# A hybrid decoder step: a buffer for each raw weight chunk of the first projection group, and the squares of later input tiles split and tied to copies of transposed columns

## The chip, the cores and the metric

The kernel runs on one core of a Trainium2 chip. The metric is the device time of one execution in microseconds (us); smaller is better. Engines are named as in the profile: PE multiplies matrices and transposes through the matrix unit, PEld loads its weights, DVE is the vector engine, ACT the activation engine, POOL the general engine, and SP issues most DMA transfers. An engine works through its own list of instructions in order, and an instruction that waits holds back all that stand behind it on that engine.

## The reference, cut to what matters

One layer of a decoder with two kinds of attention heads. Only its beginning matters here: all rows (16 learned meta tokens, 1024 prompt tokens, 32 sample tokens) are normalized and multiplied by a wide input matrix.

```python
def rms_norm(x, g):
    xf = x.astype(jnp.float32)
    var = jnp.mean(xf * xf, axis=-1, keepdims=True)
    return (xf * lax.rsqrt(var + EPS) * g.astype(jnp.float32)).astype(x.dtype)
...
    h = rms_norm(x, norm_pre_g[l])
    u = h @ w_in          # 2048 x 7184; columns 2048 on are the values "sv"
```

Everything after that (stick-breaking attention over prompt and paged cache, gated linear attention, gates, the output projection) is not touched by the change.

## The kernel before, in words

**The start.** The 1072 rows are nine tiles of up to 128 rows and 2048 columns: x0 to x7, each loaded as two halves of 1024 columns (512 KB a half, L207 and L212), and the small x8 with 112 rows (L209, L210). The halves share 11 buffers (tag "x"), so the twelfth half and later ones wait until a transposition has finished with an older half. Each tile goes through norm_x (L215): ACT squares it into a scrap area with a running sum (L225; halves of 1024 columns for x0 to x4, quarters of 512 for x5 to x7, four pieces of 256 for x8), DVE adds up the partial sums (L227), rstd_ (L156) makes the reciprocal root in a chain of one DVE operation (L162), two ACT operations (L163, L164) and four DVE operations (L165 to L168), and DVE scales both halves in place (L236).

**Three column chunks.** `CHUNKS` cuts the rows into 0 to 383, 384 to 767 and 768 to 1071, three x tiles each. For each chunk c and each of 16 blocks k of 128 columns, PE transposes three 128x128 pieces into one PSUM bank tx (L260; five banks, so the sixth waits until the first is emptied), ACT copies the bank into the high part of hT with the gain gpre (L261), and DVE subtracts to get the low part (L262), which empties the bank. hT holds the whole normalized input, transposed, for the rest of the projections.

**The first weight group.** The product with the first 128 value columns runs along with the transpositions: three matmuls for each c and k (L272 high by high, L273 low by high, L274 high by low). Its weights come as eight chunks of 256x128 (weight_chunk, L177): SP loads the raw chunk into a buffer of tag "wr" (128 KB, L180), ACT rounds it to the high part (L184), DVE subtracts to the low part (L185). Tag "wr" has 3 buffers in the pool wp, which serves the weight chunks of all later groups too, so the fourth raw chunk waits until the first has been subtracted. The next group, wr_k, uses the same tag and the inproj loop (L289 to L291).

**What sets the order.** A scheduler turns the program into one list per engine. Loads and weight chunks are marked urgent. Where the later tiles are normalized is written out by hand: `NORMS` (L238) says after which (c, k) the whole norm_x of a tile is called, for example tile 3 after (0, 1) and tile 8 after (1, 8). Transfers take turns on eight completion semaphores, so a transfer also waits until the one eight places earlier has landed. Small constants are loaded by `constants` (L139): the attention bias, nbal, a gain and the page table; DVE negates nbal once it has landed (L142).

Other names that the prediction uses: gpre (L133) is the gain, loaded through the ACT queue in 2048 elements of 4 bytes; the load of x7 on SP waits for the last transposition of chunk 0; acc_k at L289 is the first matmul after the three chunks.

Of the kernel before, what the change touches and what calls it, by code (L numbers as in the profile page):

```python
# [10 lines left out]
F32 = mybir.dt.float32  # L11
# [4 lines left out]
AF = mybir.ActivationFunctionType  # L16
# [4 lines left out]
P = 128  # L21
D = 2048
NK = D // P
# [15 lines left out]
C_SQ, C_SK, C_SV, C_SG, C_GQ, C_GK, C_GV, C_GG, C_GA = 0, 1024, 2048, 3072, 4096, 4608, 5120, 6144, 7168  # L39
# [8 lines left out]
NOSYNC = mybir.DependencyInfo(mybir.DependencyClass.NoSync, mybir.DependencyReason.DATA)  # L48
# [34 lines left out]
def hybrid_step(ctx: ExitStack, tc: tile.TileContext, x_prompt, x_sample, cache_k, cache_v, state_gla,  # L83
# [5 lines left out]
    vec, act, pool = nc.vector, nc.scalar, nc.gpsimd  # L89
# [12 lines left out]
    wp = wp_cm.__enter__()  # L102
# [29 lines left out]
    gpre = cst.tile([P, NK], F32, name="gpre")  # L132
# [39 lines left out]
    hT = [slots.tile([P, 2176], F32R, tag=f"s{k}", name=f"hT{k}") for k in range(NK)]  # L172
# [1 line left out]
    hl = [t[:, 1088:1088 + T] for t in hT]  # L174


    def weight_chunk(w, kk, c0, nm, dst=None):  # L177
        with urgent():
            raw = wp.tile([P, 2, P], F32, tag="wr", name=f"wr_{nm}")
            nc.sync.dma_start(raw[:], w[kk * 256:(kk + 1) * 256, c0:c0 + P].rearrange("(k p) c -> p k c", p=P))  # L180
            if dst is None:
                dst = [wp.tile([P, 2, P], F32R, tag=t, name=f"{t}_{nm}")[:] for t in ("wh", "wl")]
            wh, wl = dst
            act.copy(wh, raw[:])  # L184
            vec.tensor_tensor(wl, raw[:], wh.bitcast(F32), ALU.subtract)  # L185
        return wh, wl
# [3 lines left out]
    with tc.tile_pool(name="xp", bufs=2) as xp, tc.tile_pool(name="xps", bufs=5, space=PSUM) as xps:  # L190
        wf = xp.tile([P, 14, P], F32R, tag="wf", bufs=1, name="wf")
        wfl = [stg.tile([P, 2, P], F32R, tag="stg", name=f"wfl{kk}")[:] for kk in range(7)]
        first = [accp.tile([P, 512], F32, tag="acc", name=f"acc_v0_{c}") for c in range(3)]
        wchunks = []
        xts = {}

        def load_x(i):

            xt = [xp.tile([P, H], F32, tag="x", bufs=11, name=f"x{i}_{f}") for f in range(2 if i < 8 else 1)]
            if i == 8:  # L200
                pool.memset(xt[0][32:64], 0.0)
            with urgent():
                for f in range(2):
                    fs = slice(f * H, (f + 1) * H)
                    if i == 0:
                        nc.scalar.dma_start(xt[f][:META], meta_tokens[:, fs])
                        nc.sync.dma_start(xt[f][META:], x_prompt[0, 0:P - META, fs])  # L207
                    elif i == 8:
                        nc.scalar.dma_start(xt[0][64 * f:64 * f + 16], x_prompt[0, SEQ - 16:SEQ, fs])  # L209
                        nc.sync.dma_start(xt[0][64 * f + 16:64 * f + 48], x_sample.rearrange("b t d -> (b t) d")[:, fs])  # L210
                    else:
                        nc.sync.dma_start(xt[f][:], x_prompt[0, i * P - META:(i + 1) * P - META, fs])  # L212
            xts[i] = xt

        def norm_x(i):  # L215
            xt = xts[i]
            rows = P if i < 8 else 112
            w = H if i < 5 else 512 if i < 8 else 256
            q = len(xt) * H // w
            ssq = xp.tile([P, 4], F32, tag="ssq", name=f"ssq{i}")  # L220
            for e in range(q):
                j0 = 0 if i < 5 else (448 if i < 8 else 768) + 1088 * (e % 2)
                jk = hT[15][:rows, j0:j0 + w]
                xe = xt[e * w // H][:rows, e * w % H:e * w % H + w]
                act.activation(jk, xe, AF.Square, accum_out=ssq[:rows, e:e + 1])  # L225
            sq = xp.tile([P, 1], F32, tag="sq", name=f"sq{i}")
            vec.tensor_reduce(sq[:rows], ssq[:rows, :q], mybir.AxisListType.X, ALU.add)  # L227
            if i == 8:
                other = xp.tile([P, 1], F32, tag="so", bufs=1, name="so")
                pool.memset(other[:], 0.0)  # L230
                vec.tensor_copy(other[0:48], sq[64:112])
                vec.tensor_copy(other[64:112], sq[0:48])
                vec.tensor_tensor(sq[:rows], sq[:rows], other[:rows], ALU.add)
            r = rstd_(xp, sq[:rows], D, rows, 1, f"x{i}")
            for t in xt:
                vec.tensor_scalar(t[:rows], t[:rows], r, None, ALU.mult)  # L236

        NORMS = {(0, 1): 3, (0, 4): 4, (0, 10): 5, (1, 2): 6, (1, 5): 7, (1, 8): 8}  # L238
        for i in range(5):
            load_x(i)  # L240
            if i == 2:
                constants()
                for kk in range(NK // 2):
                    dst = (wf[:, 2 * kk:2 * kk + 2, :], wfl[kk]) if kk < 7 else None
                    wchunks.append(weight_chunk(w_in[0], kk, C_SV, f"v0_{kk}", dst))
        for i in range(3):
            norm_x(i)
        for c, (lo, hi) in enumerate(CHUNKS):
            n = hi - lo
            for k in range(NK):  # L250
                ps = xps.tile([P, 384], F32, tag="tx", name=f"tx{c}_{k}")
                ks = slice(k % 8 * P, (k % 8 + 1) * P)
                for j in range(3):
                    xt = xts[3 * c + j]
                    if len(xt) == 2:
                        src, ii = xt[k // 8][:, ks], ident[:]
                    else:
                        rs = slice(64 * (k // 8), 64 * (k // 8) + 48)
                        src, ii = xt[0][rs, ks], ident[rs, rs]
                    nc.tensor.transpose(ps[:, j * P:min((j + 1) * P, n)], src, ii)  # L260
                act.activation(hh[k][:, lo:hi], ps[:, :n], AF.Copy, scale=gpre[:, k:k + 1])  # L261
                vec.scalar_tensor_tensor(hl[k][:, lo:hi], ps[:, :n], gpre[:, k:k + 1], hh[k][:, lo:hi].bitcast(F32),  # L262
                                         ALU.mult, ALU.subtract)
                if c == 0 and k == 7:
                    load_x(5)
                if (c, k) in NORMS:
                    norm_x(NORMS[c, k])
            lo, hi = SCHUNKS[c]
            o_ = first[c][:, :hi - lo]
            for k in range(NK):  # L270
                wh, wl = (t[:, k % 2, :] for t in wchunks[k // 2])
                mm(o_, wh, hh[k][:, lo:hi], start=(k == 0), stop=False)  # L272
                mm(o_, wh, hl[k][:, lo:hi], start=False, stop=False)  # L273
                mm(o_, wl, hh[k][:, lo:hi], start=False, stop=(k == NK - 1))  # L274
            if c == 0:
                for i in (6, 7, 8):
                    load_x(i)
# [1263 lines left out]
```

## Time and profile before

| what | value |
|---|---|
| median of 3 runs | 2123.5 us (2121.63 to 2123.98) |
| span of the profiled execution | 2126.0 us, 2.5 us above that median; no other time of this execution is given |
| busy PE, DVE, ACT | 97%, 74%, 47% of the span |
| mean granted PE clock | 0.993 |
| first transposition on PE | 13.30 us |
| first matmul after the three chunks | 73.61 us |

The profile is read in four views. The page gives shares for the whole span. The table of stretches ("windows") gives the busy time of each engine between two times; an engine whose busy time equals the stretch is the bound there. The view of waits says which engine waited for what. The timeline lists instructions in order: start in us, duration in us, engine, line, operation, output and inputs, count when several like ones are merged, and in brackets the idle time before with what ended it. Rows marked SPq or ACTq are DMA issues, not the transfers themselves.

### The profile page before, as it was taken

What the parts mean: (1) busy time and instruction counts of PE and PEld (TensorE: products, weight loads), DVE (VectorE), ACT (ScalarE), POOL (GpSimd) and SP (SyncE); (2) the same over time, 40 slices, a digit from 0 to 9 for tenths busy, and PEclk for the clock granted to TensorE, in tenths of its full rate; (3) what the DMA queues carried; (4) which work ended last, traced back from release to release, by engine and by line L of the source; (5) the groups of instructions that cost most, each with busy time, mean ns of one, the idle gap of its engine ahead of it and who ended that gap; (6) DMA issues with size and microseconds to landing.
All of it is one profiled execution on the core that took longest, in us unless ns stands there. A gap on an engine that the chain in (4) does not pass through costs nothing.

```text
span 2126.0 us, 43346 instructions
## 1 busy us (share of the span) xinstructions
PE 2062.8 (97%) x12546; PEld 1872.1 (88%) x12546; DVE 1573.4 (74%) x6592; ACT 995.7 (47%) x2536; POOL 81.8 (4%) x298
## 2 busy tenths in 40 slices
PE   5999999999999999999999999999999999999997
PEld 5999999999999989999898998998888897777765
DVE  6368888889888889898798898978544446453575
ACT  7345556565555646434435335353444335342332
POOL 0000000100001000100000000000000000000000
PEclk9999999999999999999999999999999999999999
DMA  6234443544444354554343444335777665452484
GB/s 198 72 99 127 129 127 103 142 127 113 136 130 121 109 138 118 158 137 116 113 128 109 132 122 128 96 86 151 239 225 241 223 192 185 136 153 75 129 285 171
DMA packets 380442, 304.02 MB, mean 143 GB/s; under 512 B 50410, under 2 KB 320682, under 8 KB 380202
## 3 DMA queue, kind: packets, MB, share of 16 engines
q1 hardware_dynamic: 378010, 300.97, 49.0%
q8 instruction: 99, 1.62, 0.3%
q14 instruction: 141, 1.16, 0.2%
q10 hardware_dynamic: 2192, 0.27, 0.1%
HBM read 243.39 MB, written 57.72 MB: 142 GB/s over the span
## 4 chain that ended last, share of the span: by engine, by line
PE 82%; DVE 7%; DMA 6%; ACT 2%; issue 2%; SPq 0%; POOL 0%; ACTq 0%; DVEq 0%; POOLq 0%
PE acc_g L289 4%; PE acc_g L291 4%; PE acc_g L290 4%; PE b L1450 4%; PE b L1451 4%; PE b L1452 4%; PE acc_k L289 3%; PE acc_k L290 3%; PE acc_k L291 3%; PE acc_q L289 3%; PE acc_q L290 3%; PE acc_q L291 3%; PE acc_v L289 3%; PE acc_gv L289 3%; PE acc_gv L291 3%; PE acc_gv L290 3%
## 5 line engine op out<-in xcount | busy, mean ns | idle before, releaser
L384 DVE SCALAR_TENSOR_TENSOR jk<-kp,qb 128x128 f32<-128x128 f32 x2048 | 591.0, 289 | 39.7 <-DMA qb<-qsd 2.3
L289 PE MATMUL acc_g<-hT,wh_g 128*128 128x368 f32 (+2 forms) x768 | 251.3, 327 | 1.3 <-ACT gx L438 1.2
L291 PE MATMUL acc_g<-hT,wl_g 128*128 128x368 f32 (+2 forms) x768 | 248.0, 323 | 0.0
L290 PE MATMUL acc_g<-hT,wh_g 128*128 128x368 f32 (+2 forms) x768 | 247.6, 322 | 0.0
L1450 PE MATMUL b<-ring,f 128*128 128x512 f32 x416 | 166.7, 402 | 6.6 <-ACT gx L438 3.7
L1314 DVE TENSOR_TENSOR ring<-wr,ring 128x512 fp32r<-128x512 f32 x104 | 70.7, 690 | 134.8 <-ACT ring L1313 134.3
L384 DVE DVE_READ_ACCUMULATOR jk<-kp,qb 128x1 f32 x2048 | 166.4, 81 | 0.0
L1451 PE MATMUL b<-ring,f 128*128 128x512 f32 x416 | 163.5, 393 | 0.8 <-DVE ring L1314 0.7
L1452 PE MATMUL b<-ring,f 128*128 128x512 f32 x416 | 163.2, 392 | 0.0
L289 PEld LDWEIGHTS acc_g<-hT,wh_g 128*128 128x128 f32 x768 | 144.7, 188 | 13.1 <-issue 7.3
L291 PEld LDWEIGHTS acc_g<-hT,wl_g 128*128 128x128 f32 x768 | 144.6, 188 | 2.0 <-issue 2.0
L290 PEld LDWEIGHTS acc_g<-hT,wh_g 128*128 128x128 f32 x768 | 144.7, 188 | 0.7
L1313 ACT CAST ring<-wr 128x512 fp32r<-128x512 f32 x104 | 64.4, 622 | 163.0 <-DMA wr<-in_w_out_dram 72.9
L289 PE MATMUL acc_gv<-hT,wh_gv 128*128 128x384 f32 (+1 forms) x384 | 129.2, 337 | 0.0
L289 PE MATMUL acc_k<-hT,wh_k 128*128 128x378 f32 (+1 forms) x384 | 127.6, 332 | 0.0
L290 PE MATMUL acc_k<-hT,wh_k 128*128 128x378 f32 (+1 forms) x384 | 125.4, 326 | 0.0
L289 PE MATMUL acc_q<-hT,wh_q 128*128 128x368 f32 (+2 forms) x384 | 125.3, 326 | 0.0
L291 PE MATMUL acc_gv<-hT,wl_gv 128*128 128x384 f32 (+1 forms) x384 | 125.3, 326 | 0.0
L291 PE MATMUL acc_k<-hT,wl_k 128*128 128x378 f32 (+1 forms) x384 | 125.2, 326 | 0.0
L290 PE MATMUL acc_gv<-hT,wh_gv 128*128 128x384 f32 (+1 forms) x384 | 124.7, 325 | 0.0
L290 PE MATMUL acc_q<-hT,wh_q 128*128 128x368 f32 (+2 forms) x384 | 123.6, 322 | 0.0
L291 PE MATMUL acc_q<-hT,wl_q 128*128 128x368 f32 (+2 forms) x384 | 123.5, 322 | 0.0
(427 smaller groups left out, 5403.5 us busy)
## 6 DMA issues: line engine op xcount, KB each, us to landing
kp<-in_cache_k_dram SPq DMA_DIRECT2D x512, 64.0 KB
vr<-in_cache_v_dram SPq DMA_DIRECT2D x64, 512.0 KB
tf<-in_w_out_dram SPq DMA_DIRECT2D x64, 256.0 KB
qb<-qsd SPq DMA_DIRECT2D x64, 256.0 KB
td<-tf SPq DMA_DIRECT2D x64, 256.0 KB
wr_g<-in_w_in_dram SPq DMA_DIRECT2D x128, 128.0 KB
wr<-td SPq DMA_DIRECT2D x64, 256.0 KB
wr<-in_w_out_dram SPq DMA_DIRECT2D x48, 256.0 KB
```

Of the source, the lines that this page charges most:

```text
L289: mm(acc[c][:, :n], wh[:, k2, :], hh[k][:, lo:hi], start=(k == 0), stop=False)
L290: mm(acc[c][:, :n], wh[:, k2, :], hl[k][:, lo:hi], start=False, stop=False)
L291: W.mark = mm(acc[c][:, :n], wl[:, k2, :], hh[k][:, lo:hi], start=False, stop=(k == NK - 1)).ins
L384: ins = vec.scalar_tensor_tensor(jk[:], kp[:], 1.0, qbs[h, b][:, t, :], ALU.mult, ALU.mult, accum_out=zt[:, t, NPG - 1 - i:NPG - i])
L1313: act.copy(wh, r)
L1314: vec.tensor_tensor(wl, r, wh.bitcast(F32), ALU.subtract)
L1450: mm(bk[:], ah, wh, start=first and k == 0, stop=False, skip_group_check=True)
L1451: mm(bk[:], ah, wl, start=False, stop=False, skip_group_check=True)
L1452: mm(bk[:], al, wh, start=False, stop=last and k == 7, skip_group_check=True)
```

## The change

Two edits, both in the first 74 us. First, each raw chunk of the first weight group gets a buffer of its own: a tag "w0" with 8 buffers in the pool of the start phase, 8 KB more of each partition there; the other groups keep the 3 buffers of tag "wr". Second, the squares leave norm_x for a function of their own. Tiles 0 to 2 are squared as before. For tiles 3 to 8 a table `SQUARES` names, for each (c, k), a tile and the parts of it that are squared there, in two steps for tiles 3 to 7; each square is ordered behind the ACT copy of that (c, k), with an ordering that adds no semaphore wait, since both are on ACT. The rest of norm_x follows after the last part. Sizes of squares and their number stay the same.

```diff
-    def weight_chunk(w, kk, c0, nm, dst=None):
+    def weight_chunk(w, kk, c0, nm, dst=None, raw=None):
         with urgent():
-            raw = wp.tile([P, 2, P], F32, tag="wr", name=f"wr_{nm}")
+            if raw is None:
+                raw = wp.tile([P, 2, P], F32, tag="wr", name=f"wr_{nm}")
...
+        sums_x = {}
+
+        def squares(i, parts, behind=None):
+            xt = xts[i]
+            rows = P if i < 8 else 112
+            w = H if i < 5 else 512 if i < 8 else 256
+            if i not in sums_x:
+                sums_x[i] = xp.tile([P, 4], F32, tag="ssq", name=f"ssq{i}")
+            for e in parts:
+                j0 = 0 if i < 5 else (448 if i < 8 else 768) + 1088 * (e % 2)
+                jk = hT[15][:rows, j0:j0 + w]
+                xe = xt[e * w // H][:rows, e * w % H:e * w % H + w]
+                ins = act.activation(jk, xe, AF.Square, accum_out=sums_x[i][:rows, e:e + 1])
+                if behind is not None:
+                    tc.add_manual_dep(ins.ins, behind.ins.name, NOSYNC, reason="behind")
+
         def norm_x(i):
             xt = xts[i]
             rows = P if i < 8 else 112
-            w = H if i < 5 else 512 if i < 8 else 256
-            q = len(xt) * H // w
-            ssq = xp.tile([P, 4], F32, tag="ssq", name=f"ssq{i}")
-            for e in range(q):
-                j0 = 0 if i < 5 else (448 if i < 8 else 768) + 1088 * (e % 2)
-                jk = hT[15][:rows, j0:j0 + w]
-                xe = xt[e * w // H][:rows, e * w % H:e * w % H + w]
-                act.activation(jk, xe, AF.Square, accum_out=ssq[:rows, e:e + 1])
+            q = len(xt) * H // (H if i < 5 else 512 if i < 8 else 256)
+            ssq = sums_x.pop(i)
...
-        NORMS = {(0, 1): 3, (0, 4): 4, (0, 10): 5, (1, 2): 6, (1, 5): 7, (1, 8): 8}
+        SQUARES = {(0, 2): (3, (0,)), (0, 4): (3, (1,)), (0, 6): (4, (0,)), (0, 8): (4, (1,)), (0, 11): (5, (0, 1)), (0, 13): (5, (2, 3)),
+                   (1, 1): (6, (0, 1)), (1, 3): (6, (2, 3)), (1, 4): (7, (0, 1)), (1, 6): (7, (2, 3)), (1, 8): (8, (0, 1, 2, 3))}
         for i in range(5):
             load_x(i)
             if i == 2:
                 constants()
                 for kk in range(NK // 2):
                     dst = (wf[:, 2 * kk:2 * kk + 2, :], wfl[kk]) if kk < 7 else None
-                    wchunks.append(weight_chunk(w_in[0], kk, C_SV, f"v0_{kk}", dst))
+                    raw = xp.tile([P, 2, P], F32, tag="w0", bufs=NK // 2, name=f"wr_v0_{kk}")
+                    wchunks.append(weight_chunk(w_in[0], kk, C_SV, f"v0_{kk}", dst, raw))
         for i in range(3):
+            squares(i, (0, 1))
             norm_x(i)
...
-                act.activation(hh[k][:, lo:hi], ps[:, :n], AF.Copy, scale=gpre[:, k:k + 1])
+                moved = act.activation(hh[k][:, lo:hi], ps[:, :n], AF.Copy, scale=gpre[:, k:k + 1])
...
-                if (c, k) in NORMS:
-                    norm_x(NORMS[c, k])
+                if (c, k) in SQUARES:
+                    i, parts = SQUARES[c, k]
+                    squares(i, parts, moved)
+                    if parts[-1] == (1 if i < 5 else 3):
+                        norm_x(i)
```

What the scheduler makes of it, in the lists of the built kernel: PE, DVE and ACT differ only within the three chunks, and DVE, ACT and PE hold the same operations as before (PE in another order). On SP, raw chunks 3 to 7 now stand ahead of the second half of x3; from the loads of x6 on the list is that of before. On ACT, the casts of all eight chunks stand ahead of the first copy. On DVE, the subtractions of chunks 3 and 4 stand ahead of the scaling of x2, and those of chunks 5 to 7 ahead of the first subtraction of chunk 0 of the rows.

## The prediction

> **What bounds the kernel now.** First the head of the page: one execution, and which engine fills it.
>
> ```profile
> span 2126.0 us, 43346 instructions
> ```
>
> Then the table of stretches: length, then busy time of PE, PEld, DVE, ACT and POOL, granted PE clock, DMA share, rate.
>
> ```profile
> 13.30:25.00 11.70, 6.45 (x25) 4.79 (x25) 8.61 (x27) 7.56 (x21) 0.00 (x0) 1.00 0.85 252
> 25.00:58.00 33.00, 28.87 (x173) 26.24 (x172) 28.21 (x82) 27.34 (x79) 1.33 (x1) 0.95 0.47 124
> 58.00:73.60 15.60, 15.60 (x96) 12.52 (x94) 8.76 (x19) 8.51 (x18) 1.01 (x8) 1.00 0.00 1
> ...
> 73.60:2126.00 2052.40, 2011.86 (x12260) 1828.56 (x12258) 1525.94 (x6457) 944.74 (x2405) 78.73 (x282) 0.99 0.50 143
> ```
>
> After 73.6 us PE is busy for 2011.86 of 2052.40 us, and the lists of all engines there are unchanged. So that part moves as a block with the moment at which PE reaches it. From 58.0 to 73.6 PE is busy throughout. What the change can win or lose lies between 13.3 and 58 us, where PE idles 11.70 - 6.45 + 33.00 - 28.87 = 9.4 us, 4.1 of them after 25 us, and where PE, DVE and ACT are all near full (28.87, 28.21 and 27.34 of 33 us). I therefore follow which one is last at each step: SP, ACT, DVE, PE.
>
> SP's timeline, then its waits (total us, times, longest):
>
> ```profile
> 16.41 0.82 SPq L212 DMA_DIRECT2D x<-in_x_prompt_dram  x2
> 17.35 1.54 SPq L180 DMA_DIRECT2D wr_v<-in_w_in_dram  x3
> ...
> 26.53 1.29 SPq L212 DMA_DIRECT2D x<-in_x_prompt_dram  x3
> 27.91 2.55 SPq L180 DMA_DIRECT2D wr_k<-in_w_in_dram  x3
> ...
> 33.21 0.82 SPq L212 DMA_DIRECT2D x<-in_x_prompt_dram  x2
> ...
> 37.84 0.37 SPq L141 DMA_DIRECT2D nbal<-in_b_alpha_dram  x1
> ...
> 41.93 0.28 SPq L144 DMA_DIRECT2D pt<-in_page_table_dram  x1
> ```
>
> ```profile
> SPq L212 <- DMA gpre<-in_norm_pre_g_dram: 7.0, 1, 7.0
> ...
> SPq L335 <- DMA pt<-in_page_table_dram: 0.9, 1, 0.9
> ```
>
> At 16.41 SP has stood 7.0 us behind the landing of gpre, and then issues x3's second half. ACT's timeline:
>
> ```profile
> 20.84 1.06 ACT L225 ACTIVATE hT<-x 128x1024 fp32r<-128x1024 f32 x1 [3.55 <-DMA x<-in_x_prompt_dram]
> ...
> 21.89 1.03 ACT L261 ACTIVATE hT<-tx,gpre 128x384 fp32r<-128x384 f32 x2
> ...
> 23.85 0.70 ACT L184 CAST wf<-wr_v 128x256 fp32r<-128x256 f32 x2
> ...
> 34.78 0.83 ACT L184 CAST wh_k<-wr_k 128x256 fp32r<-128x256 f32 x2 [1.14 <-DMA wr_k<-in_w_in_dram]
> ...
> 37.51 1.04 ACT L261 ACTIVATE hT<-tx,gpre 128x384 fp32r<-128x384 f32 x2
> ...
> 38.43 0.63 ACT L225 ACTIVATE hT<-x 128x512 fp32r<-128x512 f32 x1
> ...
> 40.27 0.62 ACT L225 ACTIVATE hT<-x 128x512 fp32r<-128x512 f32 x1
> ...
> 42.32 1.52 ACT L261 ACTIVATE hT<-tx,gpre 128x384 fp32r<-128x384 f32 x3 [1.33 <-PE tx L260]
> 43.73 0.21 ACT L163 ACTIVATE r_x<-v_x 128x1 f32<-128x1 f32 x1
> 43.82 0.59 ACT L261 ACTIVATE hT<-tx,gpre 128x384 fp32r<-128x384 f32 x1
> ```
>
> The copies of chunk 0 run from 21.89 to 38.55. The four squares of x6 (first and last quoted, 38.43 and 40.27) fill a hole in which ACT would wait anyway: after them it still idles 1.33 us. DVE's timeline:
>
> ```profile
> 17.36 0.15 DVE L165 TENSOR_TENSOR t_x<-r_x 128x1 f32<-128x1 f32 x1
> ...
> 18.12 1.42 DVE L236 TENSOR_SCALAR x<-x,r_x 128x1024 f32<-128x1024 f32 x2
> ...
> 22.49 1.14 DVE L262 SCALAR_TENSOR_TENSOR hT<-tx,gpre,hT 128x384 fp32r<-128x384 f32 x2
> ...
> 24.52 0.75 DVE L185 TENSOR_TENSOR wfl<-wr_v,wf 128x256 fp32r<-128x256 f32 x2
> ...
> 39.65 1.42 DVE L236 TENSOR_SCALAR x<-x,r_x 128x1024 f32<-128x1024 f32 x2
> ...
> 43.95 0.17 DVE L142 TENSOR_SCALAR nbal<-nbal 128x4 f32<-128x4 f32 x1 [2.58 <-DMA nbal<-in_b_alpha_dram]
> 44.02 1.66 DVE L262 SCALAR_TENSOR_TENSOR hT<-tx,gpre,hT 128x384 fp32r<-128x384 f32 x3
> ...
> 47.56 1.41 DVE L236 TENSOR_SCALAR x<-x,r_x 128x1024 f32<-128x1024 f32 x2
> ...
> 51.36 1.42 DVE L236 TENSOR_SCALAR x<-x,r_x 128x1024 f32<-128x1024 f32 x2
> ...
> 57.62 0.76 DVE L236 TENSOR_SCALAR x<-x,r_x 112x1024 f32<-112x1024 f32 x1
> ```
>
> Chunk 1 starts on DVE at 44.02, held up by a small constant, nbal. From there to the scaling of x8 (done 58.38) DVE is the bound, and PE can finish chunk 2 only from then: 58.38 to 73.61 is 15.2 us of PE. PE's timeline:
>
> ```profile
> 25.45 0.52 PE L273 MATMUL acc_v<-hT,wf 128*128 128x378 f32 x1
> 25.76 0.52 PE L274 MATMUL acc_v<-hT,wfl 128*128 128x378 f32 x1
> 26.08 0.84 PE L260 MATMUL tx<-ident,x 128*128 128x128 f32 x3
> ...
> 27.84 0.49 PE L260 MATMUL tx<-ident,x 128*128 128x128 f32 x3
> ...
> 73.61 0.33 PE L289 MATMUL acc_k<-hT,wh_k 128*128 128x378 f32 x1
> ```
>
> Three transpositions take 0.84 us at 26.08 and 0.49 at 27.84: PE is slow until about 27.5. A slow matmul holds the next one back 0.31 us (25.45, 25.76, 26.08).
>
> **Part 1, a buffer for each raw chunk.** SP no longer waits for the subtraction of an older chunk. But the semaphore turns stay: chunk 3 takes the place of x3's second half behind gpre, so it is issued at 16.41 too. Each issue costs 0.51 us (1.54 / 3), so chunk 4 goes at 16.9, chunk 7 at 18.4, and x3, x4, x5 (one turn each, 0.41 us) come 2.5 us later than x3's half did.
>
> When do they land? No row shows a lone chunk. Upper bound: x3's half, 512 KB, issued at 16.41 and in use at 20.84, 4.4 us. Lower bound: the page table, 256 bytes, issued at 41.93 with a wait of 0.9 us behind its 0.28 us issue, 1.2 us. A chunk has a quarter of the half's bytes: 1.2 + (4.4 - 1.2)/4 = 2.0, and as five follow each other I take 2.4: chunk 4 at 19.3, chunk 7 at 20.8.
>
> ACT: the cast of chunk 7 (0.35 us, half of 0.70) ends near 21.2, and the first copy follows at 21.3 instead of 21.89, since the wait for x3 is no longer ahead of it. DVE: the scaling of x2 stood at 18.12 and is now behind the subtraction of chunk 4: 19.3 + 0.35 cast + 0.38 subtraction + 0.2 for the last step of the root = 20.2. Then scaling 0.71, three subtractions 1.1, the second scaling 0.71, and the first subtraction of hT at 22.7, against 22.49: **+0.2 us**. In PE's new order two slow matmuls of 0.31 us fewer stand ahead of the transposition (26.08) that frees the buffer of x5's second half, so that load is issued at 26.53 + 0.2 - 0.6 = 26.1. x3's second half, issued 2.5 us later than before, lands near 23.4; ACT asks for it after five copies and a square, at 25, so it waits for none.
>
> Rest of chunk 0 on ACT, from 21.3: 16 copies of 0.52 (8.3), four squares of 1.05 (20.84 to 21.89; 4.2), four of 0.61 (a third of 38.43 to 40.27; 2.4), two casts of wr_k (0.8), two DMA issues at SP's 0.41 (0.8) and six root steps of 0.09 (43.73 to 43.82; 0.5): 17.0, end 38.3, before 38.55. The wait for wr_k may stay: ACT comes to that cast near 33.3, and the load, 6.9 us from issue to use before (27.91 to 34.78), is issued at 27.5 and would land at 34.4. Its queue is not empty ahead of it now, so I take half of that 1.1 us: 38.9. x5's root ends there; after four DVE steps of 0.19 (17.36 to 18.12) and 0.71 of scaling, chunk 1 has its third tile at 40.4 and its first copy at 41.0. But nbal keeps its place: its issue follows the landing of x7's first half, whose load waits for the last transposition of chunk 0, and that depends on the eleventh subtraction, again near 32 us. So the load stays near 33.2 and nbal near 43.95. **Part 1 in sum: 0**, with bounds of -1.2 (0.6 us of PE and 0.6 us of the first copy both reach nbal) and +3 (chunk 7 takes the upper bound of 4.4 us, +2.0, and the whole wait for wr_k stays).
>
> **Part 2, the squares.** Those of x3 to x5 only change places within a busy ACT. Those of x6 leave the hole at 38.43 and come after the copies 1 and 3 of chunk 1. ACT from the first copy, 41.0: five copies of 0.52 and four squares of 0.61 are 5.0, then the root's first step, at 46.2; one square of x7 stands between its two ACT steps, so the second is done at 47.0. DVE is there too by then, with five subtractions from 44.02 on (0.55 each) and the two small steps ahead of the root. But the four steps that follow now stand in a row, 0.19 each with nothing between them, to 47.8, and x6 is scaled by 49.2. Before, x6 is scaled at 48.97 (47.56 + 1.41) with six subtractions ahead of it in the list; now at 49.2 with five: 0.55 + 0.2 = 0.8 later. For x7 likewise: one ACT step stands behind a square of x8, which costs between 0 and the 0.61 of a wider one; I take 0.4: **+1.2 us** at x8's scaling (57.62 becomes 58.8). PE has no slack there: chunk 1's matmuls follow the same subtractions. Bounds: 0, if ACT gets so far ahead while DVE waits for nbal that the roots are ready, and 1.6, if both roots cost 0.8.
>
> **Sum.** 0 + 1.2: the profiled 2126.0 us becomes 2127.2. The median lies 2.5 below, and 2123.5 becomes 2124.7.
>
> **Rivals.**
>
> *PE at full rate earlier.* For: the slow rate ends near 27.5, and without ACT's wait for x3 PE has hardly a hole between the transpositions of x2 and the matmuls. From the end of the first subtraction (22.49 + 0.57) to the transposition at 26.08 are 3.0 us, 2.4 in the new order; at the fast rate 1.2. Then x5's load, wr_k, x7 and nbal come up to 1.2 earlier, and with the +1.2 of part 2 the time is 2123.5. Against: one execution can't show whether the hole matters. The Trainium skill ("TensorE: Matmul & The Clock Gate", Part 1) says that a busy window of about 3.4 us releases the clock, and that this window runs freely. By that rule the rival comes true in some executions; the trace agrees in that 0.84 becomes 0.49 at once.
>
> *Late chunks, slower by over 0.2%.* Place: the scaling of x2 on DVE, behind the subtraction of chunk 4, and all copies, behind the cast of chunk 7. If chunk 7 takes 1.2 us more than the upper bound (4.4), it lands at 24.0 instead of 20.8; the copies and PE start 3 us later, and 3 + 1.2 is 4.2 us, the point from which it decides. At 5.5 us in all the time is 2129. For: gpre, 8 KB in small pieces, held SP until 16.41, so bytes aren't all, and a chunk consists of pieces of 512 bytes. Against: three chunks issued from 17.35 on behind two halves of 512 KB were all landed when ACT cast the last two at 23.85.
>
> *The holes close.* If copies flow from 21.3 and PE loses none of the 4.1 us after 25, 4.1 + 0.6 go: 2118.8. Against: DVE and ACT have 28.21 and 27.34 of 33 us busy there and lose no operation.
>
> *The buffers do nothing.* Semaphore turns hold chunk 3 until 16.41 whatever buffer it has; the forecast contains that.
>
> **How the numbers follow.** 0.2% is 4.2 us, about what a measurement of this kernel can tell from no change. Forecast (0 to +4.2 us) 0.63; PE earlier (0 to -4.2) 0.21; late chunks (beyond +4.2) 0.13; holes closed (beyond -4.2) 0.03. So faster 0.03, same 0.84, slower 0.13. The range takes -1.2 for part 1, 0 for part 2 and 1.2 for the spread of the runs (half of 2121.63 to 2123.98): 2121.1. Upwards +3 and +1.6: 2128.1.
>
> **What would show it.** Right: in the changed profile chunk 3 of wr_v issued right behind gpre near 16.4; the first copy near 21.3; nbal on DVE within 1 us of 43.95; the four DVE steps of x6's root in a row; x8 scaled near 58.8; L289 on PE first at 74.8. Wrong: L289 before 73 or after 77, x6 scaled before 48.5, or a change after 73.6 us beyond that shift.

## The result and the profile after

| | before | after |
|---|---|---|
| first comparison, 8 runs each | 2123.35 us | 2128.18 us (2126.09 to 2132.3) |
| ratio, 95% interval | | 1.0026 [1.0017, 1.0035] |
| the same two once more (a1_after: 35 and 12 runs) | 2125.45 us | 2128.4 us, ratio 1.0017 [1.0008, 1.0025] |
| profiled execution: span (time) | 2126.0 us | 2127.0 us (2128.68) |
| first acc_k matmul in it | 73.61 us | 75.52 us |

The change makes the kernel slower, by 0.17 to 0.26%. Time and span of the profiled execution after differ by 1.7 us, so the profiled execution of before took about 2127.7 us, some 4 us more than its median, and not the 2.5 that the prediction carried along. It is no outlier, though: 35 later executions of before ran from 2121.66 to 2130.37 us. The medians of after agree (2128.18 and 2128.4); that of before lies between 2123.35 and 2127.48 us in the six sessions on record. Two executions of the cut kernels below ran slow and are left out of their rows: 156.32 us in s_buffers and 127.38 us in s_nbal_before.

The head of the page, and the table of stretches of the kernel after (columns as in the prediction):

```profile
span 2127.0 us, 43341 instructions
```

```profile
13.30:25.00 11.70, 6.03 (x23) 4.35 (x23) 9.28 (x27) 7.43 (x20) 0.00 (x0) 1.00 0.82 226
25.00:58.00 33.00, 26.75 (x162) 22.41 (x161) 26.84 (x77) 27.28 (x80) 0.95 (x1) 1.00 0.47 133
58.00:73.60 15.60, 15.60 (x94) 12.45 (x93) 10.19 (x23) 8.50 (x18) 0.70 (x3) 1.00 0.00 1
73.60:2127.00 2053.40, 2012.87 (x12273) 1828.97 (x12271) 1525.81 (x6459) 943.69 (x2405) 79.29 (x287) 0.99 0.49 143
```

From 25 to 58 us PE shows 162 matmuls in 26.75 us where it showed 173 in 28.87, although its granted clock is now 1.00 there and was 0.95. What PE lacks it does later, and the block that follows starts at 75.52. SP, then ACT, then DVE of the kernel after:

```profile
16.27 2.42 SPq L181 DMA_DIRECT2D wr_v<-in_w_in_dram  x5
...
37.54 0.37 SPq L141 DMA_DIRECT2D nbal<-in_b_alpha_dram  x1
```

```profile
21.59 1.51 ACT L275 ACTIVATE hT<-tx,gpre 128x384 fp32r<-128x384 f32 x3
...
34.45 0.40 ACT L185 CAST wh_k<-wr_k 128x256 fp32r<-128x256 f32 x1 [1.41 <-DMA wr_k<-in_w_in_dram]
34.76 0.20 ACT L164 ACTIVATE r_x<-r_x 128x1 f32<-128x1 f32 x1
...
38.83 0.20 ACT L163 ACTIVATE r_x<-v_x 128x1 f32<-128x1 f32 x1 [0.94 <-DVE v_x L162]
...
42.01 1.05 ACT L275 ACTIVATE hT<-tx,gpre 128x384 fp32r<-128x384 f32 x2 [2.41 <-PE tx L274]
42.95 0.63 ACT L228 ACTIVATE hT<-x 128x512 fp32r<-128x512 f32 x1
...
47.57 0.19 ACT L164 ACTIVATE r_x<-r_x 128x1 f32<-128x1 f32 x1
```

```profile
37.13 1.42 DVE L247 TENSOR_SCALAR x<-x,r_x 128x1024 f32<-128x1024 f32 x2
38.46 0.15 DVE L238 TENSOR_REDUCE sq<-ssq 128x1 f32<-128x4 f32 x1
...
40.83 1.41 DVE L247 TENSOR_SCALAR x<-x,r_x 128x1024 f32<-128x1024 f32 x2
43.27 0.17 DVE L142 TENSOR_SCALAR nbal<-nbal 128x4 f32<-128x4 f32 x1 [1.02 <-DMA nbal<-in_b_alpha_dram]
43.35 1.14 DVE L276 SCALAR_TENSOR_TENSOR hT<-tx,gpre,hT 128x384 fp32r<-128x384 f32 x2
44.78 1.14 DVE L276 SCALAR_TENSOR_TENSOR hT<-tx,gpre,hT 128x384 fp32r<-128x384 f32 x2 [0.30 <-ACT hT L275]
46.47 0.16 DVE L238 TENSOR_REDUCE sq<-ssq 128x1 f32<-128x4 f32 x1 [0.55 <-ACT hT L228]
...
47.79 0.16 DVE L165 TENSOR_TENSOR t_x<-r_x 128x1 f32<-128x1 f32 x1 [0.23 <-ACT r_x L164]
...
48.56 1.42 DVE L247 TENSOR_SCALAR x<-x,r_x 128x1024 f32<-128x1024 f32 x2
53.25 1.42 DVE L247 TENSOR_SCALAR x<-x,r_x 128x1024 f32<-128x1024 f32 x2
59.51 0.75 DVE L247 TENSOR_SCALAR x<-x,r_x 112x1024 f32<-112x1024 f32 x1
```

Two places are new. **In chunk 0** x4's root (ACT L164 at 34.76) stands behind the cast of wr_k, which waits 1.41 us for its load. DVE scales x4 at 37.13 (before: 32.54), only then sums x5's squares (38.46), and ACT waits 0.94 us for that sum at 38.83. **In chunk 1** ACT idles 2.41 us ahead of the first copy, the hole that x6's squares used to fill; then it squares x6 between copies, and DVE waits 0.30, 0.55 and 0.23 us for ACT until x6 is scaled at 48.56.

### The profile page after: what moved, and what is told of

It reads as the page before. It is cut to its first block, busy times and chain, and to the rows that moved or that the text cites. A ratio compares the mean times of both kernels' runs of the same rounds, so it can differ in the third digit from the quotient of the medians.

```text
span 2127.0 us, 43341 instructions
## 1 busy us (share of the span) xinstructions
PE 2061.5 (97%) x12546; PEld 1868.4 (88%) x12546; DVE 1574.3 (74%) x6592; ACT 994.7 (47%) x2536; POOL 81.7 (4%) x298
## 4 chain that ended last, share of the span: by engine, by line
PE 81%; DVE 8%; DMA 6%; issue 2%; ACT 2%; SPq 1%; DVEq 0%; ACTq 0%
PE acc_g L306 5%; PE acc_g L308 5%; PE acc_g L307 5%; PE b L1467 4%; PE b L1468 4%; PE b L1469 4%; PE acc_k L306 3%; PE acc_k L307 3%; PE acc_k L308 3%; PE acc_q L306 3%; PE acc_q L307 3%; PE acc_q L308 3%; PE acc_v L306 3%; PE acc_v L307 3%; PE acc_v L308 3%; PE acc_gv L306 2%
## 5 line engine op out<-in xcount | busy, mean ns | idle before, releaser
L306 PE MATMUL acc_k<-hT,wh_k 128*128 128x378 f32 (+1 forms) x384 | 127.6, 332 | 0.0
```

What stands on the lines that cost most here:

```text
L306: mm(acc[c][:, :n], wh[:, k2, :], hh[k][:, lo:hi], start=(k == 0), stop=False)
```

## The experiments

Before the experiments ran, three theories were set against each other. Theory A says that the whole loss is made before the first acc_k matmul, by late squares; B, that part of it lies behind that matmul; C, that the buffers cost.

### First set: the parts, in the whole kernel

c0_before is the kernel before, unchanged. e1_buffers adds the buffers alone:

```diff
-                    wchunks.append(weight_chunk(w_in[0], kk, C_SV, f"v0_{kk}", dst))
+                    raw = xp.tile([P, 2, P], F32, tag="w0", bufs=NK // 2, name=f"wr_v0_{kk}")
+                    wchunks.append(weight_chunk(w_in[0], kk, C_SV, f"v0_{kk}", dst, raw))
```

e2_squares is the kernel after without these two lines. e3_hole is the kernel after with x6's squares called between chunk 0 and chunk 1:

```diff
-                   (1, 1): (6, (0, 1)), (1, 3): (6, (2, 3)), (1, 4): (7, (0, 1)), (1, 6): (7, (2, 3)), (1, 8): (8, (0, 1, 2, 3))}
+                   (1, 4): (7, (0, 1)), (1, 6): (7, (2, 3)), (1, 8): (8, (0, 1, 2, 3))}
...
+                if (c, k) == (1, 2):
+                    norm_x(6)
...
             if c == 0:
                 for i in (6, 7, 8):
                     load_x(i)
+                squares(6, (0, 1, 2, 3), moved)
```

c0_before: 

> The kernel before once more, for a second trace and as a control. Theory A (all of the loss is made before the first matmul behind the three chunks): ratio 1.000; this trace reaches that matmul between 71.5 and 74 us, so at least 1.5 us ahead of the 75.5 of the changed kernel, and the stretch after it is as long as the changed kernel's, 2051.5 us, within 1.5 us. Rival B (part of the loss lies after that matmul): ratio 1.000 too, but the stretch after it is 2049 us or less.

e1_buffers: 

> Only the eight buffers, norms where they were before. Theory A, squares cost and buffers don't: -0.7 to +0.7 us against before, ratio 0.9997 to 1.0003. Rival C (the buffers cost, through the casts that stand ahead of the first copy and the scaling of x2 behind two of them): +3 to +5 us, ratio 1.0015 to 1.0024.

e2_squares: 

> Only the moved squares, three buffers as before. Theory A: chunk 1 has the roots of x6 and x7 late as in the changed kernel, +2.5 to +4.5 us, ratio 1.0012 to 1.0021, and the scaling of x8 comes about 16 us after the first subtraction of chunk 1 (13.6 before, 16.2 in the changed kernel). Rival C: 0 to +1 us.

e3_hole: 

> The changed kernel, but the four squares of x6 stand between the copies of chunk 0 and chunk 1, in the hole where ACT waits, and the rest of its norm after copy 2 of chunk 1 as before. Theory A: most of the loss of chunk 1 goes, the scaling of x8 comes 14 to 15 us after the first subtraction of chunk 1, and the time is -0.5 to +1.5 us against before, ratio 0.9998 to 1.0007. Rivals B and C: the loss stays, +3 to +5 us, ratio 1.0015 to 1.0024.

| kernel | ratio to before | acc_k in its trace |
|---|---|---|
| c0_before | 0.9994 [0.9985, 1.0003] | 73.31 |
| e1_buffers | 1.0002 [0.9992, 1.0012] | 74.00 |
| e2_squares | 1.0007 [0.9998, 1.0016] | 75.96 |
| e3_hole | 1.0017 [1.0008, 1.0027] | 76.62 |

c0_before comes out as A has it: acc_k at 73.31, and 2052.7 us from there to the end, where B wanted 2049 or less (one trace, of a stretch that varies by 8 us over the ten traces of whole kernels). The buffers alone cost nothing that shows, which speaks against C. But e1_buffers is not simply one half of the change: its list on SP has nbal ahead of the loads of x7, so that DVE negates nbal at 39.38, inside chunk 0, and does not wait for it at chunk 1. e2_squares has A's late acc_k, but its ratio of 1.0007 lies below A's 1.0012, and its interval reaches down to no change. e3_hole missed: no gain. In its trace the load of wr_k comes late (ACT waits 2.33 us for it) and chunk 0 ends later; x8 is scaled sooner after chunk 1's first subtraction, but only because its root moved ahead of subtractions that still have to be done: from there to acc_k it is 17.6 us instead of 16.0. But an interval here is 2 us to either side, as wide as what is asked: 35 executions of the kernel before, with one list of instructions, ran from 2121.66 to 2130.37 us.

### Second set: the same question from both sides

a1_after is the kernel after, unchanged. e6_chunk1_old has its buffers and its table for x3 to x5, but squares and normalizes x6, x7 and x8 in one call each as before; e7_chunk1_new is the mirror, the kernel before (3 buffers) with only the entries for chunk 1. Both diffs are against the kernel after:

```diff
-                   (1, 1): (6, (0, 1)), (1, 3): (6, (2, 3)), (1, 4): (7, (0, 1)), (1, 6): (7, (2, 3)), (1, 8): (8, (0, 1, 2, 3))}
+                   }
+        NORMS = {(1, 2): 6, (1, 5): 7, (1, 8): 8}
...
+                if (c, k) in NORMS:
+                    squares(NORMS[c, k], (0, 1, 2, 3))
+                    norm_x(NORMS[c, k])
```

```diff
-        SQUARES = {(0, 2): (3, (0,)), (0, 4): (3, (1,)), (0, 6): (4, (0,)), (0, 8): (4, (1,)), (0, 11): (5, (0, 1)), (0, 13): (5, (2, 3)),
-                   (1, 1): (6, (0, 1)), (1, 3): (6, (2, 3)), (1, 4): (7, (0, 1)), (1, 6): (7, (2, 3)), (1, 8): (8, (0, 1, 2, 3))}
+        NORMS = {(0, 1): 3, (0, 4): 4, (0, 10): 5}
+        SQUARES = {(1, 1): (6, (0, 1)), (1, 3): (6, (2, 3)), (1, 4): (7, (0, 1)), (1, 6): (7, (2, 3)), (1, 8): (8, (0, 1, 2, 3))}
...
+                if (c, k) in NORMS:
+                    i = NORMS[c, k]
+                    squares(i, (0, 1) if i < 5 else (0, 1, 2, 3))
+                    norm_x(i)
```

e4_nbal_before is the kernel before with nbal negated behind the three chunks and ordered behind the last subtraction there (`low`, L262):

```diff
-        vec.tensor_scalar(nbal[:], nbal[:], -1.0, None, ALU.mult)
...
+    ins = vec.tensor_scalar(nbal[:], nbal[:], -1.0, None, ALU.mult)
+    tc.add_manual_dep(ins.ins, low.ins.name, NOSYNC, reason="behind")
```

a1_after: 

> The changed kernel once more, beside the kernel before on the same chip, since the first comparison (1.0026, interval 1.0017 to 1.0035, that is +3.6 to +7.4 us) is larger than what the two traces show (first acc_k matmul at 75.52 instead of 73.61, +1.9 us, and a stretch after it of 2051.5 instead of 2052.4). Theory A (the whole loss is made before that matmul, and the rest of the first comparison is spread of the executions): acc_k starts between 75.2 and 75.9 again, and the ratio lies near 1.0009 (1.0003 to 1.0016). Theory B (some of the loss lies behind that matmul, though the lists there are the same): acc_k starts at the same time, but the ratio is 1.0020 or more again.

e6_chunk1_old: 

> The changed kernel with its 8 buffers and its table for tiles 3 to 5, but tiles 6 to 8 are squared and normalized in one call each, after columns 2, 5 and 8 of chunk 1 as in the kernel before; the four squares of x6 so fall back into the hole ahead of chunk 1's first copy. Theory A (the loss comes from the squares of x6 and x7 that are ordered behind chunk 1's copies): acc_k starts at 73.3 to 74.2, x8 is scaled 13.6 us after chunk 1's first subtraction as before, and the ratio is 0.9998 to 1.0004. Theory C (the order in chunk 0 or the buffers cost as well): acc_k starts at 75 or later and the ratio is 1.0008 or more.

e7_chunk1_new: 

> The mirror of the run before it: the kernel before with its 3 raw buffers and its tiles 3 to 5 as they were; only the squares of tiles 6 to 8 are split and ordered as in the changed kernel. Theory A: x8 is scaled 16 us after chunk 1's first subtraction, 2.5 us more than before, so acc_k starts at 75.3 to 76.2 and the ratio is 1.0008 to 1.0013. Theory C: acc_k starts below 74.3 and the ratio is within 1.0004.

e4_nbal_before: 

> The kernel before, with the negation of nbal on DVE moved behind the last subtraction of chunk 2, where its value is not yet needed. It takes away the 2.58 us for which DVE waits for nbal ahead of chunk 1's first subtraction. Theory A (the time is set by where DVE is with chunk 1, so the wait moves everything behind it): chunk 1's first subtraction starts at 42.7 instead of 44.0, the next limit being ACT's first copy at 42.3, and acc_k starts about 1.2 us earlier, at 72.2 to 72.7, ratio 0.9994. Rival (DVE makes up for the wait, because later subtractions wait for ACT and PE anyway): acc_k stays at 73.3 to 73.7, ratio 1.0000.

| kernel | ratio to before | acc_k in its trace |
|---|---|---|
| a1_after | 1.0017 [1.0008, 1.0025] | 75.86 |
| e6_chunk1_old | 1.0004 [0.9996, 1.0013] | 76.52 |
| e7_chunk1_new | 1.0009 [0.9999, 1.0019] | 75.81 |
| e4_nbal_before | 0.9995 [0.9986, 1.0003] | 72.73 |

e7_chunk1_new and e4_nbal_before come out as theory A has them, in ratio and trace (72.73 a hair beyond 72.7). a1_after has A's trace, but its ratio lies between A and B and decides neither. e6_chunk1_old contradicts itself: its ratio says no loss, its trace 3 us; that trace is of the slowest of its 12 executions (2131.1 us). The cast of the last raw chunk, in its trace:

```profile
23.64 0.40 ACT L185 CAST wh_v<-wr_v 128x256 fp32r<-128x256 f32 x1 [2.54 <-DMA wr_v<-in_w_in_dram]
```

In the trace of the kernel after that cast begins at 21.28. One trace of a start like this can be off by 2 us through a single late transfer. Whoever compares two starts needs many executions of the start alone.

### Third set: the start alone

The kernels are cut off after head 0's values, keys and queries, so that some 127 us remain; the lists of ACT, DVE and SP up to acc_k stay as they were.

```diff
-            V = values(h)
-            W.spawn(attend(h, qt, kt, V), 2)
...
-        for h in range(HEADS):
+        head(0)
+        W.flush()
...
```

(and nothing after it). s_before, s_after, s_buffers and s_squares are the kernels before, after, e1_buffers and e2_squares, cut.

s_before: 

> The kernel before, cut off after the first three groups (values, keys and queries of head 0); everything after that is left out, so most outputs are not computed, and its time is compared only with the three cut kernels beside it. The lists of the engines up to the first acc_k matmul are those of the whole kernel. It measures the start in many executions, without the spread of the 2050 us behind it. Expected of every theory: acc_k starts at 73.3 to 73.7 as in both traces of the whole kernel. Theory A adds that the times of its executions lie within about 1 us; theory D (the start itself varies by several us from execution to execution, so that single traces mislead) that they spread over 3 us or more.

s_after: 

> The changed kernel, cut off in the same way. Theory A: acc_k starts at 75.5 to 75.9, and the median is 1.9 to 2.4 us above that of the cut kernel before. If the change's loss of 3 to 5 us in the whole kernel were already made in the start (theory D), the median would be 3 us or more above. If it is 2 us here, anything beyond that in the whole kernel lies after the start (theory B) or is spread.

s_buffers: 

> The kernel before with the 8 raw buffers alone, cut off in the same way. Theory A: the buffers cost about what one trace of the whole kernel showed, 0.4 to 0.7 us above the cut kernel before. Theory C (the buffers cost): 1.5 us or more.

s_squares: 

> The kernel before with the moved squares alone and 3 raw buffers, cut off in the same way. Theory A: 2.3 to 2.7 us above the cut kernel before, as the one trace of the whole kernel had it (75.96 instead of 73.3 to 73.6), that is as much as the whole change or a little more. Theory C: under 1 us.

| kernel | median (range) | above s_before |
|---|---|---|
| s_before | 127.05 us (126.67 to 127.31) | |
| s_after | 130.44 us (130.22 to 131.21) | 3.4 |
| s_buffers | 127.11 us (126.68 to 127.58) | 0.1 |
| s_squares | 130.21 us (129.79 to 131.32) | 3.2 |

The ranges of s_before and s_buffers overlap, those of s_squares and s_after overlap, and 2.2 us lie between the two pairs. **The start loses 3.4 us, and the squares make it: they cost 3.2 us alone, and the buffers add 0.2 to them.** C has fallen as the cause. In s_squares nbal comes early too (issued at 30.50), but with the squares moved it is not what holds DVE, as the fourth set shows. That s_buffers costs next to nothing is luck. In s_buffers, on DVE (x5, then x6):

```profile
40.45 1.42 DVE L237 TENSOR_SCALAR x<-x,r_x 128x1024 f32<-128x1024 f32 x2
...
45.80 1.42 DVE L237 TENSOR_SCALAR x<-x,r_x 128x1024 f32<-128x1024 f32 x2
```

x5 is scaled 1.4 us later than in s_before (39.09, below), but nbal is issued at 32.27 instead of 36.72 and no longer holds DVE at chunk 1, so that x6 comes at the same time (45.73 in s_before). The two cancel.

3.4 us of 2123 are 0.16%, inside the interval of a1_after (+1.7 to +5.3 us) and just below that of the first comparison (+3.6 to +7.4 us). B is not needed for the second comparison (a1_after); that some of the first is lost after acc_k can't be excluded. D, that the start varies by 3 us or more, isn't borne out by these ranges, but A's forecasts missed too: the loss is 3.4 and not 1.9 to 2.4, s_squares loses 3.2 and not 2.3 to 2.7, and s_before starts acc_k at 71.80 and not at 73.3 to 73.7. The traces show where. s_before, DVE and the first acc_k:

```profile
32.06 1.41 DVE L236 TENSOR_SCALAR x<-x,r_x 128x1024 f32<-128x1024 f32 x2
...
39.09 1.42 DVE L236 TENSOR_SCALAR x<-x,r_x 128x1024 f32<-128x1024 f32 x2
...
42.12 0.17 DVE L142 TENSOR_SCALAR nbal<-nbal 128x4 f32<-128x4 f32 x1 [1.31 <-DMA nbal<-in_b_alpha_dram]
...
45.73 1.42 DVE L236 TENSOR_SCALAR x<-x,r_x 128x1024 f32<-128x1024 f32 x2
...
49.53 1.42 DVE L236 TENSOR_SCALAR x<-x,r_x 128x1024 f32<-128x1024 f32 x2
...
55.80 0.75 DVE L236 TENSOR_SCALAR x<-x,r_x 112x1024 f32<-112x1024 f32 x1
```

```profile
71.80 0.33 PE L289 MATMUL acc_k<-hT,wh_k 128*128 128x378 f32 x1
```

s_after, the same:

```profile
40.89 1.42 DVE L247 TENSOR_SCALAR x<-x,r_x 128x1024 f32<-128x1024 f32 x2
43.05 0.17 DVE L142 TENSOR_SCALAR nbal<-nbal 128x4 f32<-128x4 f32 x1 [0.74 <-DMA nbal<-in_b_alpha_dram]
...
48.62 1.42 DVE L247 TENSOR_SCALAR x<-x,r_x 128x1024 f32<-128x1024 f32 x2
...
53.32 1.42 DVE L247 TENSOR_SCALAR x<-x,r_x 128x1024 f32<-128x1024 f32 x2
...
59.58 0.76 DVE L247 TENSOR_SCALAR x<-x,r_x 112x1024 f32<-112x1024 f32 x1
```

```profile
75.57 0.33 PE L306 MATMUL acc_k<-hT,wh_k 128*128 128x378 f32 x1
```

s_after runs like the whole kernel after. s_before runs 1.8 us ahead of the trace on which the prediction stands (nbal 42.12 instead of 43.95). ACT's first use of x3 and SP's issues in s_before:

```profile
19.93 1.06 ACT L225 ACTIVATE hT<-x 128x1024 fp32r<-128x1024 f32 x1 [3.06 <-DMA x<-in_x_prompt_dram]
```

```profile
25.62 1.47 SPq L212 DMA_DIRECT2D x<-in_x_prompt_dram  x3
...
32.67 0.82 SPq L212 DMA_DIRECT2D x<-in_x_prompt_dram  x2
...
36.72 0.37 SPq L141 DMA_DIRECT2D nbal<-in_b_alpha_dram  x1
```

In the trace of before these stand at 20.84, 26.53, 33.21 and 37.84: x3 landed 0.9 us later, every load behind it was issued later, nbal 1.1 us, and nbal then took another 0.7 us longer to land (43.95 - 37.84 against 42.12 - 36.72). It is no single accident: the four whole kernels with the chunk 0 of before (before, c0_before, e7_chunk1_new, e4_nbal_before) issue nbal at 37.3 to 37.8 in their traces, their three cut forms at 36.2 to 36.7. The kernel after does so at 37.5 and 37.6 whole and at 37.0 and 37.8 cut. Which of the two the untraced whole executions resemble isn't seen, and the time of an execution doesn't tell it: the trace of e7_chunk1_new, with nbal issued at 37.49, is of the fastest of its 12 executions (2124.18 us). By their ratios the two whole comparisons are +5.5 and +3.6 us, nearer to the 3.4 of the cut kernels than to the 1.9 and 2.5 between whole traces. So the trace of before may have been late, by up to 1.8 us at nbal, and may have hidden that much of the loss. But all four whole traces with that chunk 0 are late, so it may as well be that the cut kernels start earlier, and that the start of the whole kernel loses some 2 us. The runs don't decide this.

### Fourth set: where the squares lose it, and what nbal has to do with it

The cut forms of e7_chunk1_new, e6_chunk1_old, e4_nbal_before, and of the kernel after with nbal negated late, the same edit as in e4. Theory A2: in the kernel before DVE, held by nbal, is the bound of chunk 1; in the kernel after it is ACT. Rival E: the entries for chunk 0 make the loss.

s_chunk1_new: 

> Cut like the others: the kernel before with only the squares of x6 to x8 split and ordered behind copies of chunk 1. Theory A2 (ACT becomes the bound of chunk 1, since x6's four squares leave the hole ahead of it): from the first copy, still at 40.3, ACT needs 5.75 us to the end of x6's root as in the cut changed kernel, so x6 is scaled from 47.0 instead of 45.7, x7's root costs another 0.9, and the median is 2.0 to 2.6 us above the cut kernel before (129.0 to 129.7). Rival E (the chunk-0 part of the table makes the loss): 1 us or less.

s_chunk1_old: 

> Cut like the others: the buffers and the moved squares of x3 to x5, with tiles 6 to 8 normalized in one call each as before. Theory A2: x5 is scaled at 40.9 instead of 39.1, but the wait for nbal hides half of that; chunk 1's first subtraction is at 43.1 instead of 42.2 and x8 is scaled 13.6 us after it as before, so the median is 0.7 to 1.2 us above the cut kernel before (127.8 to 128.3). Rival E: 2.5 us or more.

s_nbal_before: 

> Cut like the others: the kernel before with the negation of nbal behind the last subtraction of chunk 2. Theory A2 (in the kernel before DVE, held by nbal, is the bound of chunk 1): the 1.31 us of waiting go, the first subtraction starts at 40.9, and the median is 0.9 to 1.3 us below the cut kernel before (125.8 to 126.2). Rival (the wait is made up for later): within 0.3.

s_nbal_after: 

> The same for the changed kernel. Theory A2 (there ACT is the bound of chunk 1, with x6's root done at 47.8 whatever nbal does): the first subtraction starts 0.4 us earlier, x6 is scaled at 48.6 as before, and the median is within 0.3 us of the cut changed kernel (130.1 to 130.7). Rival (DVE, held by nbal, is the bound there too, as the prediction assumed): 0.4 to 0.7 us below it.

| kernel | median (range) | difference |
|---|---|---|
| s_chunk1_new | 129.32 us (128.44 to 129.91) | +2.3 to s_before |
| s_chunk1_old | 128.25 us (127.6 to 129.5) | +1.2 to s_before |
| s_nbal_before | 125.7 us (125.07 to 125.83) | -1.3 to s_before |
| s_nbal_after | 131.27 us (130.61 to 132.51) | +0.8 to s_after |

The two halves add up: 2.3 for chunk 1 and 1.2 for chunk 0 with the buffers are 3.5, and 3.4 was measured. That agreement is coarse, since these rows and s_before come from two sessions, and the same cut kernel differs by 0.5 us between sessions (s_after and s_after2). Both rows lie where A2 has them. E falls as the main cause, but chunk 0 with the buffers makes a third of the loss. Without the wait for nbal the kernel before gains the 1.3 us for which it waited; that its first subtraction starts at 40.9 isn't seen, since its trace is of the execution that is left out. The last row missed its forecast, so the same two kernels ran once more, side by side.

s_after2: 

> The cut changed kernel once more, as the neighbour of the next run. Theory A2: 130.2 to 131.0 us, x6 scaled 6.5 to 6.6 us after chunk 1's first copy.

s_nbal_after2: 

> The cut changed kernel with the late negation of nbal, beside its neighbour. Theory A2 (nbal is not the bound there, ACT is): within 0.3 us of the neighbour. Rival (the late negation costs something itself, perhaps through the moved place in DVE's list): 0.5 us or more above it.

130.96 us (130.83 to 131.28) against 130.88 (130.2 to 131.15): the late negation changes nothing in the kernel after that these ranges can show; most of the 0.8 lay between two sessions (s_after2 is itself 0.5 above s_after). The sharpest number is the distance from chunk 1's first copy on ACT to the scaling of x6 on DVE. From s_nbal_after2, where no nbal stands in the way:

```profile
42.60 1.05 ACT L274 ACTIVATE hT<-tx,gpre 128x384 fp32r<-128x384 f32 x2 [2.42 <-PE tx L273]
```

```profile
49.16 1.42 DVE L246 TENSOR_SCALAR x<-x,r_x 128x1024 f32<-128x1024 f32 x2
```

That is 6.56 us. It is 6.55 in s_after (42.07 to 48.62) and 6.56 in s_after2, s_nbal_after and s_chunk1_new. In s_before it is 5.39 (40.34 to 45.73), with DVE held by nbal for 1.31 us of that. In e4_nbal_before, with the old squares and nothing that holds DVE, it is 4.18:

```profile
42.11 1.52 ACT L260 ACTIVATE hT<-tx,gpre 128x384 fp32r<-128x384 f32 x3 [1.32 <-PE tx L259]
```

```profile
46.29 1.42 DVE L235 TENSOR_SCALAR x<-x,r_x 128x1024 f32<-128x1024 f32 x2
```

So the moved squares lengthen it by 2.4 us, four squares of 0.61, and with them it is fixed by ACT, whatever nbal does. The old squares with nbal negated late beat both kernels, in the cut form by 1.3 us against before; in the whole kernel the 0.9995 [0.9986, 1.0003] of e4_nbal_before can't be told from no change.

## Why the prediction was wrong, point by point

- **"Those of x3 to x5 only change places within a busy ACT": the step that failed.** The prediction put this term at nothing; s_chunk1_old, with the buffers and this part of the table, costs 1.2 us. The working counted ACT's sum and not what stands behind what. In the trace of the kernel after, the third tile of chunk 1 is ready at 41.5 (40.83 and half a scaling) where the working had 40.4, and the first copy is at 42.01 instead of 41.0. x4's second square moved behind a later copy, and x4's root fell behind the cast of wr_k. The wait there was 1.41 us, where the working took half of 1.1, and ACT then waited 0.94 us for DVE's sum of x5, a wait that the working doesn't have. How the 1.2 us divide between the squares and the buffers isn't separated: x5 is scaled at 40.89 in s_after, at 40.56 with the squares alone and at 40.45 with the buffers alone, against 39.09 in s_before.
- **Part 2, the squares in chunk 1: mechanism right, size wrong for x6.** The four root steps stand in a row and x6 and x7 come late, as forecast. The stretch of ACT was well judged: from the first copy to x6's scaling 6.8 us by the working (41.0 to 47.8), 6.55 measured. The 0.8 us for x6 are 0.2 on the clock and 0.55 for the subtraction that now stands behind it. By the same count x6 loses 1.35 us in s_chunk1_new (46.53 against 45.73, and 0.55) and 1.55 in the trace of the kernel after (48.56 against 47.56, and 0.55). x7 adds 0.34 in both, where 0.4 were taken. In the medians, 1.2 us became 2.3 (s_chunk1_new).
- **What this gives in the profiled pair.** x8 is scaled at 59.51 instead of the 58.8 forecast, and L289 starts at 75.52 instead of 74.8: 1.9 us where 1.2 were forecast. The 0.7 between them are, nearly, the 1.0 us of the first copy less the 0.25 by which ACT was quicker.
- **Before's own trace as the measure.** Part 2 sets x6 scaled at 49.2 against 48.97, which rests on nbal at 43.95 in one execution of before. There DVE was held so long that little was left for ACT to lose. With nbal at 42.12, as in s_before, x6 is done at 47.15 (45.73 + 1.42), and the kernel after, where ACT is the bound, gains nothing from an earlier nbal: s_after has acc_k at 75.57, the whole kernel after 75.52. So the same change costs 1.9 us against that trace and 3.8 against the trace of s_before. Which of the two the whole kernel has stays open.
- **Part 1, buffers: right for the kernel after.** Chunk 3 is issued at 16.27 behind gpre (forecast 16.4), the first copy is at 21.59 (21.3), nbal at 43.27 (within 1 us of 43.95). Beside the squares the buffers cost 0.2 us (forecast 0). With the buffers alone the time agrees by luck: the first copy is at 23.60 in s_buffers, since x3's square still stands ahead of it, and nbal is out of the way.
- **"PE at full rate earlier": fell.** Three transpositions take 0.49 us from 26.65 on instead of 27.84 in the kernel after, and nothing was gained: PE shows 11 matmuls fewer between 25 and 58 us, and x5's second half was issued at 26.1 as that rival wants, but nbal only 0.3 us earlier (37.54).
- **"Late chunks": fell as the cause.** In the trace of the kernel after the last chunk is cast at 21.28, and the first copy follows at once. A single execution has it (23.64 in e6_chunk1_old).
- **"The holes close": fell.** ACT idles 2.41 us ahead of chunk 1's first copy where it idled 1.33, and 0.94 more before that.
- **After 73.6 us: right**, as far as it can be seen: 2051.5 us from acc_k to the end instead of 2052.4, where ten traces lie between 2046.6 and 2055.0.
- **The sum.** 1.2 us were forecast; 1.9 came between the profiled executions, 3.4 between the cut kernels, 4.8 and 2.9 between the medians of the two whole comparisons. 2123.5 + 3.4 is 2126.9, inside the range; the measured 2128.18 lies 0.08 us above it, and the 1.4 us between 3.4 and 4.8 stay open, within that comparison's spread. With a loss so near to the prediction's own 4.2 us, "same" at 0.84 was far too sure: by their ratios one comparison lies beyond that point and one within. The range came from one trace's bounds, and the spread of the median was set at 1.2 us when executions differ by 9.

## What to carry to other kernels

Before an instruction is moved, ask what stood still while it ran: squares that filled a hole were free, and between copies they cost their full time. Before a wait in one trace is taken as a fixed point, trace it again; the time of the execution doesn't tell whether its start was late. Before a part is tested alone, see what else it moves: with the buffers alone, nbal changed its place and hid what they cost. When a change touches 70 us of 2100, cut the kernel: five executions of the start told more than 35 of the whole. But run the pair side by side, and see whether the cut start runs as the whole one does.

## What the runs showed of the hardware

The clock of PE halved for 3.4 us in one execution and not in another with the same list: the kernel after ran at 1.00 from 44.4 to 47.8 us in its first trace and at 0.51 in that of a1_after. The kernel before has such a stretch too, and s_before doesn't. Stretch 37.8 to 41.2 us in the trace of before, then in s_before (columns as above):

```profile
37.80:41.20 3.40, 3.40 (x15) 3.14 (x14) 3.31 (x10) 3.19 (x10) 0.00 (x0) 0.51 1.08 187
```

```profile
37.80:41.20 3.40, 3.11 (x22) 2.62 (x20) 2.91 (x9) 3.40 (x11) 0.00 (x0) 1.00 0.84 135
```

This is where the 0.95 of the prediction's stretch 25 to 58 us comes from (3.4 of 33 us at 0.51): 15 matmuls at half clock against 22. With it chunk 1's first copy stands at 42.32 (s_before 40.34), but nbal at 43.95 covers that. All four whole traces with the chunk 0 of before have such a stretch, between 36 and 41.4 us. The Trainium skill ("TensorE: Matmul & The Clock Gate", Part 1) says that the gate's window is 3.4 us and runs freely; the length agrees. It also says that the gate closes after an idle window; here the longest pauses of PE between 25 us and this stretch were 1.55 us in the trace of before and 1.53 in s_before, where the clock stayed at 1.00.

```profile
36.15 0.44 PE L272 MATMUL acc_v<-hT,wf 128*128 128x378 f32 x1 [1.55 <-ACT hT L261]
```

```profile
35.59 0.44 PE L272 MATMUL acc_v<-hT,wf 128*128 128x378 f32 x1 [1.53 <-ACT hT L261]
```

And the same raw chunk, loaded by the same list on SP, was cast at 21.28 us in one execution and at 23.64 in another.
